# Cross-entropy over 256 x 32000 logits: another order of the row groups and other sizes of the first loads

## The chip, the cores and the metric

The kernel runs on one core of one Trainium2 chip. The metric is the device time of one execution in microseconds (us). Three executions of the kernel before took 82.39, 82.45 and 82.46 us, median 82.45 us.

## The reference

```python
def setup_inputs():
    batch, num_classes = 256, 32000
    return {
        "logits": np.random.randn(batch, num_classes).astype(np.float32),
        "labels": np.random.randint(0, num_classes, size=batch).astype(np.int32),
    }

def reference(logits, labels):
    log_probs = logits - np.max(logits, axis=-1, keepdims=True)
    log_probs = log_probs - np.log(np.sum(np.exp(log_probs), axis=-1, keepdims=True))
    return np.array([-log_probs[i, labels[i]] for i in range(batch)]).astype(np.float32)
```

For each of the 256 rows the result is log(sum of exp(row)) minus the logit at the row's label. The logits are 32.77 MB of float32, and each of them is read once.

## The kernel before

**Groups and loads.** The 256 rows are cut into four consecutive groups (`GROUPS`, L18). A group of k rows is spread over all 128 partitions: each row is cut into q = 128/k equal pieces, and each piece takes one partition, so that a group of 128 rows has 32000 columns per partition, one of 64 rows has 16000 and one of 32 rows has 8000. All groups together have 64000 columns per partition, and one such column over 128 partitions is 512 bytes. Each group is loaded in a few pieces of consecutive columns (`LOADS`, L20). The loads are numbered through all groups, x0 to x13; x8 to x13 lie side by side in one tile, `x_tail`.

**Buffers.** x0 to x5 each have a buffer of their own (`SLOTS`, L30), and their loads are issued at the start, one after the other, on SP's queue (`load`, L204 to L206). x0's load is moved ahead of the barrier at the program's start. x6 and x7 use the buffers of two earlier loads again, and `x_tail` (`TAIL_SLOT`, L32) that of a third one. Their loads are issued on the same queue, each once the work on the buffer's former contents is over. The order is written out by hand: the loop at L307 to L312 places each later load behind the steps that free its buffer.

**Steps.** For each load, `step` (L270) runs `exps` (L215) on ACT: an exponential in place over the whole load, 128 partitions x its columns. What sums its result differs:

- For the loads of the first group, ACT sums along the row itself, into one column of `parts`. After the group's last load, DVE adds these columns (L284), and a matmul with the group's columns of `weights` brings the 128 partition sums to one sum per row (L285).
- For the loads in `HALVED` (L41: x2 to x11), DVE adds the two halves of the result and sums them (L294), and a matmul adds that to the group's sums (L300).
- For the last two, x12 and x13, ACT sums itself again, and the matmul at L300 follows directly.

**Weights.** `weights` says which partitions belong to which row, each entry times exp(-logit at the label). The logits at the labels are gathered by indirect DMAs near the start (L250); the exponential of them (L274) is placed on ACT behind the exponential of load number `GATHERED` (L39), and L276 to L282 make the weights from it. The logarithm of weights times sums is then the result itself.

**End.** The logarithms (`logs`, L222) run on ACT: that of the first group behind the second group's first exponential, those of the middle groups and of the last group at the end, from two banks of PSUM. Then SP stores the 256 results (L318). 16 matmuls whose result is not used (L291, `WARM`) are placed behind the exponential of x7.

Of the kernel before, what the change touches and what calls it, by code (L numbers as in the profile page):

```python
# [14 lines left out]

GROUPS = [64, 128, 32, 32]  # L18

LOADS = [  # L20
    [2048, 13952],
    [8896, 8192, 8320, 6592],
    [4736, 3264],
    [2496, 1824, 1344, 992, 736, 608],
]
CHUNKS = [n for ns in LOADS for n in ns]
GROUP_OF = [g for g, ns in enumerate(LOADS) for _ in ns]


SLOTS = [0, 1, 2, 3, 4, 5, 2, 3]  # L30
TAIL = len(SLOTS)
TAIL_SLOT = 1  # L32
SKIP = 32


WARM_FROM = 7
WARM = 16

GATHERED = 1  # L39

HALVED = range(2, 12)  # L41


def begin_first_load_before_barrier(nc):
# [72 lines left out]
def kernel(  # L117
# [9 lines left out]
    B, C = logits.shape  # L127
    assert B == P * ROWS == sum(GROUPS)
    row_at = [sum(GROUPS[:g]) for g in range(len(GROUPS) + 1)]
    for k, ns in zip(GROUPS, LOADS):  # L130
        assert P % k == 0 and sum(ns) * P == k * C
    assert C % (P // min(GROUPS)) == 0


    flat = [
        logits[row_at[g]:row_at[g + 1], :].rearrange("k (q c) -> (k q) c", q=P // k)
        for g, k in enumerate(GROUPS)
    ]
    starts = [sum(ns[:j]) for ns in LOADS for j in range(len(ns))]
    first_of = [GROUP_OF.index(g) for g in range(len(GROUPS))]  # L140
    last_of = [first_of[g] + len(ns) - 1 for g, ns in enumerate(LOADS)]
# [6 lines left out]
    width = {}  # L148
    for i, s in enumerate(SLOTS):
        width[s] = max(width.get(s, 0), CHUNKS[i])  # L150
    width[TAIL_SLOT] = max(width[TAIL_SLOT], sum(CHUNKS[TAIL:]))


    place = []
    for i, s in enumerate(SLOTS):
        skip = SKIP if s == 0 else 0
        t = big.tile([P, skip + width[s]], F32, name=f"x{i}", tag=f"slot{s}")
        place.append(t[:, skip:skip + CHUNKS[i]])
    assert all(width[s] % 64 == 0 for s in width)
    tail = big.tile([P, width[TAIL_SLOT]], F32, name="x_tail", tag=f"slot{TAIL_SLOT}")  # L160
    for i in range(TAIL, last + 1):
# [3 lines left out]

    assert HALVED[0] == last_of[0] + 1 and HALVED[-1] == last - 2
    assert all(CHUNKS[i] % 2 == 0 for i in HALVED)
    parts = small.tile([P, len(LOADS[0])], F32, name="parts")
    row_0 = small.tile([P, 1], F32, name="row_0")
    near = {i: small.tile([P, 1], F32, name=f"near{i}") for i in range(HALVED[0], last + 1)}  # L170
    res = small.tile([1, B], F32, name="res")
# [36 lines left out]
    def exps(i):  # L208
        if i in HALVED:
            acc = None  # L210
        elif i > last_of[0]:
            acc = near[i][:, :]
        else:
            acc = parts[:, i:i + 1]
        nc.scalar.activation(out=place[i], in_=place[i], func=AF.Exp, accum_out=acc)  # L215
# [8 lines left out]
    with tc.manual_schedule():  # L224
        first = len(set(SLOTS))
        for i in range(first):
# [43 lines left out]
        def step(i):  # L270
            exps(i)
            g = GROUP_OF[i]
            if i == GATHERED:
                nc.scalar.activation(out=eg[:, :], in_=g_at[:, :], func=AF.Exp, scale=-1.0)  # L274
                for r in range(ROWS):
                    nc.vector.tensor_scalar_mul(diag[r][:, :], ident[:, :], eg[:, r:r + 1])  # L276

                for r in range(ROWS):
                    nc.tensor.matmul(  # L279
                        spread[:, r * P:(r + 1) * P], ones[:, :], diag[r][:, :], start=True, stop=True  # L280
                    )
                nc.vector.tensor_mul(out=weights[:, :], in0=holds[:, :], in1=spread)  # L282
            if i == last_of[0]:
                nc.vector.reduce_sum(out=row_0[:, :], in_=parts[:, :], axis=mybir.AxisListType.X)  # L284
                nc.tensor.matmul(lane[0], row_0[:, :], weigh(0), start=True, stop=True)  # L285
            if i == last_of[0] + 1:
                logs(slice(0, row_at[1]), lane[0])
            if i == WARM_FROM:
                col = place[i][:, CHUNKS[i] - 1:CHUNKS[i]]
                for _ in range(WARM):  # L290
                    nc.tensor.matmul(warm, col, diag[0][:, :], start=True, stop=True)  # L291
            if i in HALVED:
                half = CHUNKS[i] // 2
                nc.vector.scalar_tensor_tensor(  # L294
                    out=place[i][:, 0:half], in0=place[i][:, 0:half], scalar=1.0,
                    in1=place[i][:, half:CHUNKS[i]],
                    op0=mybir.AluOpType.mult, op1=mybir.AluOpType.add, accum_out=near[i][:, :],
                )
            if g:
                nc.tensor.matmul(  # L300
                    lane[g], near[i][:, :], weigh(g), start=i == first_of[g], stop=i == last_of[g]
                )


        assert GATHERED <= last_of[0]
        done = 0
        for i in range(first, last + 1):  # L307
            slot = SLOTS[i] if i < TAIL else TAIL_SLOT
            while done <= SLOTS[:first].index(slot):
                step(done)  # L310
# [40 lines left out]
```

## Time and profile before

| what | value |
|---|---|
| median of the three executions | 82.45 us |
| profiled execution, its own time | 82.39 us |
| its span, first to last instruction | 80.8 us |
| busy: ACT, DVE, PE | 57.5, 27.6, 11.6 us |
| the 32.77 MB of the logits' queue, as a share of 16 DMA engines' span | 95.1% |
| exponential of 128x13952, 128x8896, 128x608 | 11829, 7601, 693 ns |
| starts of the exponentials of x1, x3, x4, x5 | 21.27, 41.42, 51.23, 59.02 us |
| DVE's half additions at L294, all ten | 25.9 us |

Times within a profile count from the start of its span. The time of the profiled execution is 1.6 us above its span, for what lies around the instructions. In a group's line, after the name of the operation and its shapes, stand the number of its instructions, then their busy time and the mean duration of one, and then the idle time of the engine just ahead of them with the work that ended it. In the chain of work that ended last, each piece is released by the one before it.

### The profile page before, as it was taken

The numbers are of one execution on the slowest core, as the hardware profiler recorded it, in microseconds if no ns is written. First come the engines' busy times: TensorE is split into PE (matmuls) and PEld (weight loads), VectorE is DVE, ScalarE is ACT, GpSimd is POOL, SyncE is SP. The second block draws the span as 40 slices with busy tenths as digits, with TensorE's granted clock in tenths as the row PEclk, the third lists the DMA queues.
The fourth block names the chain that finished last, engine by engine and source line by source line (L and its number), as shares of the span: only waits on it lengthen the run. The fifth ranks groups of instructions, "written<-read, shape, count | busy, mean of one in ns | idle before, by whom it ended". The sixth has DMA issues, their size and how long they took to land.

```text
span 80.8 us, 261 instructions
## 1 busy us (share of the span) xinstructions
PE 11.6 (14%) x66; PEld 6.3 (8%) x66; DVE 27.6 (34%) x28; ACT 57.5 (71%) x23; POOL 5.2 (6%) x20
## 2 busy tenths in 40 slices
PE   0040000000000000240000200020000201159961
PEld 0040000000000000220000000000000000036630
DVE  1020000000000000220079509920099198898870
ACT  6063000000499999999979990699979999999993
POOL 4006950000000000000000000000000000000000
PEclk9999999999999999999999999999999999999999
DMA  5988989999969798998998996999999999999940
GB/s 134 580 387 359 442 387 442 442 442 442 564 282 564 317 529 373 406 519 373 406 527 346 445 527 290 444 457 444 413 413 422 421 427 421 420 415 420 407 179 1
DMA packets 2084, 32.77 MB, mean 406 GB/s; under 512 B 290, under 2 KB 291, under 8 KB 932
## 3 DMA queue, kind: packets, MB, share of 16 engines
q1 hardware_dynamic: 2018, 32.77, 95.1%
q0 software_dynamic: 64, 0.00, 0.1%
q10 hardware_dynamic: 2, 0.00, 0.0%
HBM read 32.77 MB, written 0.00 MB: 406 GB/s over the span
## 4 chain that ended last, share of the span: by engine, by line
DMA 61%; ACT 34%; SPq 2%; another core or an unknown queue 1%; issue 1%; PE 0%
DMA x<-in_logits_dram 61%; ACT x L215 24%; ACT x_tail L215 9%; SPq L206 2%; PE bank L300 0%; ACT res L222 0%
## 5 line engine op out<-in xcount | busy, mean ns | idle before, releaser
L215 ACT ACTIVATE x<-x 128x2048 f32<-128x2048 f32 (+7 forms) x8 | 48.1, 6032 | 21.1 <-DMA x<-in_logits_dram 21.1
L294 DVE SCALAR_TENSOR_TENSOR x<-x 128x4448 f32<-128x4448 f32 (+5 forms) x6 | 21.8, 3631 | 16.1 <-ACT x L215 16.1
L276 DVE TENSOR_SCALAR diag<-ident,eg 128x128 f32<-128x128 f32 x2 | 0.5, 286 | 27.4 <-ACT eg L274 27.4
L300 PE MATMUL bank<-weights,near 128*1 128x32 f32 (+1 forms) x24 | 3.7, 262 | 34.4 <-DVE x L294 33.2
L215 ACT ACTIVATE x_tail<-x_tail 128x2496 f32<-128x2496 f32 (+5 forms) x6 | 7.5, 1304 | 0.0
L291 PE MATMUL bank<-diag,x 128*1 128x128 f32 x32 | 5.6, 355 | 0.0
L279 PE MATMUL bank<-diag,ones 128*128 128x128 f32 x4 | 1.2, 461 | 27.9 <-DVE diag L276 27.9
L294 DVE SCALAR_TENSOR_TENSOR x_tail<-x_tail 128x1248 f32<-128x1248 f32 (+3 forms) x4 | 4.1, 1025 | 0.6 <-ACT x_tail L215 0.3
L300 PEld LDWEIGHTS bank<-weights,near 128*1 128x1 f32 x24 | 1.0, 82 | 37.2 <-DVE x L294 35.5
L291 PEld LDWEIGHTS bank<-diag,x 128*1 128x1 f32 x32 | 3.4, 107 | 2.0
L279 PEld LDWEIGHTS bank<-diag,ones 128*128 128x128 f32 x4 | 0.9, 324 | 28.0 <-DVE diag L276 28.0
L250 POOL DMA_INDIRECT g_at<-in_logits_dram,idx x2 | 2.1, 1030 | 0.6 <-issue 0.3
L198 ACT ACT_TABLE_LOAD x1 | 1.3, 1283 | 0.8 <-PEq L335 0.8
L239 PE MATMUL bank<-one,lbl_row 1*128 1x1 f32 x4 | 1.0, 352 | 4.8 <-DVE lbl_row L237 4.8
L237 DVE CAST lbl_row<-words 1x256 f32<-1x256 int32 x1 | 0.3, 281 | 3.4 <-DMA words<-in_labels_dram 3.4
L239 PEld LDWEIGHTS bank<-one,lbl_row 1*128 1x128 f32 x4 | 0.9, 316 | 4.8 <-DVE lbl_row L237 4.8
L265 POOL TENSOR_SCALAR_AFFINE_SELECT holds<-holds 128x32 f32<-128x32 f32 (+2 forms) x4 | 1.0, 238 | 0.3
L261 POOL TENSOR_SCALAR_AFFINE_SELECT holds<-holds 128x32 f32<-128x32 f32 (+2 forms) x4 | 1.0, 238 | 0.1
L282 DVE TENSOR_TENSOR weights<-holds,bank 128x256 f32<-128x256 f32 x1 | 0.4, 420 | 1.2 <-PE bank L279 1.2
L222 ACT ACTIVATE res<-bank 1x64 f32<-1x64 f32 (+2 forms) x3 | 0.7, 219 | 0.1
L242 DVE CAST lbl<-bank 128x2 int32<-128x2 f32 x1 | 0.2, 159 | 1.1 <-PE bank L239 1.1
L294 DVE DVE_READ_ACCUMULATOR x<-x 128x1 f32 x6 | 0.5, 83 | 0.0
(18 smaller groups left out, 3.7 us busy)
## 6 DMA issues: line engine op xcount, KB each, us to landing
x<-in_logits_dram SPq DMA_DIRECT2D x1, 6976.0 KB, 20.4
x<-in_logits_dram SPq DMA_DIRECT2D x1, 4448.0 KB, 30.6
x<-in_logits_dram SPq DMA_DIRECT2D x1, 4160.0 KB, 48.9
x<-in_logits_dram SPq DMA_DIRECT2D x1, 4096.0 KB, 39.7
x<-in_logits_dram SPq DMA_DIRECT2D x1, 3296.0 KB, 56.2
x<-in_logits_dram SPq DMA_DIRECT2D x1, 2368.0 KB
x<-in_logits_dram SPq DMA_DIRECT2D x1, 1632.0 KB, 15.6
x_tail<-in_logits_dram SPq DMA_DIRECT2D x1, 1248.0 KB
```

The lines of the kernel that those rows point to most:

```text
L198: nc.scalar.preload_act_table_set("natural_log_exp_and_others")
L206: nc.sync.dma_start(out=place[i], in_=flat[GROUP_OF[i]][:, a:a + CHUNKS[i]])
L215: nc.scalar.activation(out=place[i], in_=place[i], func=AF.Exp, accum_out=acc)
L222: nc.scalar.activation(out=res[0:1, rows], in_=sums, func=AF.Ln)
L239: nc.tensor.matmul(lbl_up[:, r:r + 1], lbl_row[:, r * P:(r + 1) * P], one[:, :], start=True, stop=True)
L250: nc.gpsimd.indirect_dma_start(out=g_at[:, r:r + 1], out_offset=None, in_=logits[:, :], in_offset=bass.IndirectOffsetOnAxis(ap=idx[:, r:r ...
L261: nc.gpsimd.affine_select(out=h, in_=h, pattern=[[-q, k]], base=0, channel_multiplier=1, compare_op=mybir.AluOpType.is_ge, fill=0.0,)
L265: nc.gpsimd.affine_select(out=h, in_=h, pattern=[[q, k]], base=q - 1, channel_multiplier=-1, compare_op=mybir.AluOpType.is_ge, fill=0.0,)
L279: nc.tensor.matmul(spread[:, r * P:(r + 1) * P], ones[:, :], diag[r][:, :], start=True, stop=True)
L291: nc.tensor.matmul(warm, col, diag[0][:, :], start=True, stop=True)
L294: nc.vector.scalar_tensor_tensor(out=place[i][:, 0:half], in0=place[i][:, 0:half], scalar=1.0, in1=place[i][:, half:CHUNKS[i]], op0=mybir. ...
L300: nc.tensor.matmul(lane[g], near[i][:, :], weigh(g), start=i == first_of[g], stop=i == last_of[g])
```

## The change

The group of 128 rows comes first, ahead of the one of 64. The first group thus has four loads instead of two, 1024, 5120, 12992 and 12864 columns, and the second group two instead of four. There are 14 loads as before. The first six have 48000 columns together in both kernels. `HALVED` begins at x4 instead of x2: ACT sums for x0 to x3, and DVE has eight halves to add instead of ten. x6 takes the buffer of x1, x7 that of x3 as before, and `x_tail` that of x2. The logits at the labels are taken in behind x2's exponential. The sizes of the loads of the later groups change by little. Of the functions nothing changes.

```diff
-GROUPS = [64, 128, 32, 32]
+GROUPS = [128, 64, 32, 32]

 LOADS = [
-    [2048, 13952],
-    [8896, 8192, 8320, 6592],
-    [4736, 3264],
-    [2496, 1824, 1344, 992, 736, 608],
+    [1024, 5120, 12992, 12864],
+    [9216, 6784],
+    [4608, 3392],
+    [2560, 1824, 1312, 960, 736, 608],
 ]
...
-SLOTS = [0, 1, 2, 3, 4, 5, 2, 3]
+SLOTS = [0, 1, 2, 3, 4, 5, 1, 3]
 TAIL = len(SLOTS)
-TAIL_SLOT = 1
+TAIL_SLOT = 2
...
-GATHERED = 1
-
-HALVED = range(2, 12)
+GATHERED = 2
+
+HALVED = range(4, 12)
```

## The prediction

> **What bounds the kernel now.** I began with the page's slices and its chain of waits.
>
> ```profile
> ACT  6063000000499999999979990699979999999993
> DMA  5988989999969798998998996999999999999940
> DMA x<-in_logits_dram 61%; ACT x L215 24%; ACT x_tail L215 9%; SPq L206 2%; PE bank L300 0%; ACT res L222 0%
> ```
>
> The last line says whose work the chain consists of: loads, then ACT. The DMA row is full almost from end to end; ACT's is full only from the 11th slice on, with one hole. The chain in order of time shows where the one hands over to the other.
>
> ```profile
> 51.23 7.14 ACT x L215
> 58.37 0.62 another core or an unknown queue
> 59.02 5.62 ACT x L215
> 64.68 3.88 ACT x L215
> 68.74 2.91 ACT x L215
> 71.64 7.46 ACT x_tail L215 x8
> 79.15 0.23 PE bank L300 x2
> 79.41 0.19 ACT res L222
> ```
>
> From 59.02, the start of x5's exponential, ACT runs without a pause to the end; ahead of it ACT waited 0.62 us for x5's load. So the end is x5's landing plus what ACT has left. Two stretches of the windows view confirm that both are full at once there.
>
> ```profile
> 1.00:77.90 76.90, 11.05 (x60) 6.09 (x60) 27.05 (x26) 55.76 (x18) 4.87 (x16) 1.00 1.00 426
> 59.02:77.90 18.88, 7.27 (x46) 3.99 (x46) 15.69 (x15) 18.88 (x8) 0.00 (x0) 1.00 0.99 416
> ```
>
> The columns are stretch, length, busy time of PE, its weight load, DVE, ACT and POOL, clock, share of the DMA engines, GB/s. The DMA engines are busy from 1.00 to 77.90 (share 1.00), and ACT is busy for all 18.88 us of the second stretch. The groups by shape give durations and releasers.
>
> ```profile
> L215 ACT ACTIVATE x<-x 128x13952 f32<-128x13952 f32 x1 | 11.8, 11829 | 14.6 <-DMA x<-in_logits_dram 14.6
> L215 ACT ACTIVATE x<-x 128x8896 f32<-128x8896 f32 x1 | 7.6, 7601 | 0.0
> L215 ACT ACTIVATE x<-x 128x8320 f32<-128x8320 f32 x1 | 7.1, 7137 | 2.8 <-DMA x<-in_logits_dram 2.8
> L294 DVE SCALAR_TENSOR_TENSOR x<-x 128x4448 f32<-128x4448 f32 x1 | 4.8, 4793 | 5.3 <-ACT x L215 5.3
> L215 ACT ACTIVATE x_tail<-x_tail 128x608 f32<-128x608 f32 x1 | 0.7, 693 | 0.0
> ```
>
> ACT's pauses are ended by loads, never by DVE; DVE waits for ACT.
>
> **Two rates.** The exponentials that a load released start at 21.27 (16000 columns loaded by then), 41.42 (33088), 51.23 (41408) and 59.02 (48000). That is 1.179, 1.179 and 1.182 ns per column: the stream takes 1.18 ns. ACT takes (7601 - 693)/(8896 - 608) = 0.8335 ns per column. From the start of 8896 (33.19 in the timeline) to the next instruction (40.70) is 7.51 us, 0.10 above 8896 columns. An accumulator read adds 0.09 (33.01 to 33.10).
>
> **What costs nothing.** DVE loses the halves of x2 and x3, 4.8 and 4.4 us, and PE their two matmuls; ACT's work never waits for them, so this is worth 0. x6 no longer waits on SP for DVE at 45.66 but for x1's exponential, at about 14; behind it on SP's queue x7 waits for x3's exponential, at about 51, not for DVE until 52.95; the tail's loads stand behind that. The stream reaches x7 only after 52608 columns, at about 64.5, so 13 us cover both; with that cover gone each us late would be a us at the end. x2 lands at about 24.97 and takes 11.03 with its read, plus 0.09 for L274: ACT is free at 36.1, 4 us ahead of x3. The weights and the first group's matmul move to 51.1 to 52; the logarithm that needs them comes at 58.8. DVE adds x4's halves (4608 columns, about 5 us) while x5's exponential takes 5.8, and stays within ACT's pace from there; its last half ends about 0.8 us ahead of ACT's last sum. The middle logarithm has 96 columns instead of 160. By the rows of 64 and 160 (196 and 276 ns) that is 0.05 less, but it ended at 79.28 and the last logarithm had to wait for PE until 79.38: saved 0.
>
> **ACT from x3 on.** x3 comes with 32000 columns: 41.42 - 1088 x 1.18 ns = 40.14. Its 12864 columns and read take 11.83 (21.27 to 33.10, for 13952) less 0.91 = 10.92, to 51.06. x4 (41216 columns) lands at 51.00, so a pause of 2.78 us is used up and ACT is 0.06 behind. x4 takes 7.51 + 320 x 0.8335 ns = 7.78, to 58.84. The first group's logarithm, now 128 columns and placed here, takes 0.25 by the rows above, less the 0.09 by which ACT's instructions overlap: 59.00. x5 lands at 59.02 as before (48000 columns). Three pauses of before (2.78, 0.65 and 0.53) are down to 0.02.
>
> **ACT from x5 on.** 22784 columns instead of 22592: 192 x 0.8335 ns = +0.16. One thing goes: from x5's start to x6's was 5.66, which is 0.17 above its columns, where the next two have 0.11 and 0.09. The chain shows why: x6's load (52736 columns, about 64.6) came as ACT became free. Now x6 has 52608 columns and lands 0.15 earlier while ACT comes 0.1 later: -0.06. The sum is +0.10.
>
> **Two terms that can only add.** First, the chain x3, x4, logarithm, x5 has no room left: any landing of x3 a little late against x5's, or a dearer logarithm, is at once at the end. Bounds: 0, and 0.2 (the 0.09 overlap not had and the 0.1 by which a rate of 1.182 in place of 1.179 shifts 32000 columns). I take 0.05, near the lower end, since the three rates agree that well. Second, the start: the first load carries 1024 columns, 1.21 us of stream, instead of 2.42. It is issued at 0.00, the next at 0.80, behind the barrier. If the second's data follow its issue as fast as the first's (1.00 us; the windows view shows no byte before), there is no gap, with 0.4 us to spare; where it is slower by more, all of the stream and so the end is late. The trace never shows this delay without a backlog. Bounds: 0, and 1.2 if all of the cover is lost. The nearest row is the first load's own start, so I take 0.04.
>
> The Trainium skill (DMA: Bandwidth & Descriptors, Bandwidth) asks for 1 MiB or more per DMA to reach 75% of the peak, measured there for loads issued from GpSimd, which speaks against a first load of 0.5 MiB. By its fixed 2.0 us for a DMA (Anatomy of one DMA), of which the first load's transfer would cover 1.2, an estimate from it would be 0.8 more, 83.4. In this trace the tail's loads of 368 to 912 KB, queued back to back, ran at 420 and 407 GB/s (the slices from 72.7 to 76.8 us), so I count no such loss.
>
> **Sum.** 0.10 + 0.05 + 0.04 = +0.19. The profiled execution's 82.39 (80.8 of span and 1.6 around it) becomes 82.58; the median is 0.06 above it, so 82.64, or 0.23% more. About 0.2% (0.16 us) is what a measurement can tell from no change.
>
> **Rivals.**
> - *A gap in the stream at the start.* The second load's data come more than 0.4 us later after its issue than the first's did. For it: SP's issues take 0.33, 0.42 and 0.62 us one after the other, so the queue is slower under load. Against it: the shares at 2.0 to 3.0 us are 0.94 and 0.98 right after a start. It gives 82.8 to 83.7, most likely below 83.
> - *The stream runs ahead: not slower.* Between the first landing (4.68) and x1's (21.27) it took 1.189 ns per column; at 1.179 those 13952 columns would take 0.14 less. The place is the stream up to x3, and it decides from 0.03 us on: with x3's exponential starting ahead of 40.11 and x5's ahead of 59.0, the whole chain to the end moves with it. It gives 82.50, in its far part (0.4 us of stream gained) 82.25. For it: only that one stretch; against it: the stretch holds the start itself, and the later rates are the same for pieces of 128-row and 64-row groups.
> - *The bare sum.* Both adding terms are nil, and the end moves by the 0.10 alone: 82.55, within 0.2%. For it: each link closes by the rows above, if only just.
>
> **How the numbers follow.** Forecast (a sum of +0.17 to +0.3): 0.40. Gap: 0.15. Stream ahead: 0.25, of which 0.17 within 0.2% and 0.08 beyond. Bare sum: 0.20, of which 0.15 within and 0.05 faster, should the tail also hide the 192 columns and more. Slower 0.40 + 0.15 = 0.55, same 0.17 + 0.15 = 0.32, faster 0.08 + 0.05 = 0.13. The range takes the near part of the gap and the near part of the stream's gain: 82.38 to 82.98. The forecast's own is 82.62 to 82.75.
>
> **What would show it.** Right: x3 starts near 40.14; x4, the logarithm and x5 follow with pauses of under 0.1; x5 starts at 59.02 to 59.1; the last exponential starts at 78.4 to 78.55 instead of 78.31; the DMA share is near 1.00 from 1.0 to 77.9. A gap: slices with little DMA between 2 and 4 us and all starts late by the same amount. Stream ahead: x3 and x5 both early. Wrong altogether: a pause of ACT after x5, ended by a load or by DVE.

## The result, and the profile after

The changed kernel takes 82.94 us (median of four executions, 82.78 to 83.08), the kernel before beside it 82.43 us (82.39 to 82.46). The ratio is 1.0062, with a 95% interval of 1.0039 to 1.0085: slower by 0.51 us. The forecast was 82.64 in a range of 82.38 to 82.98. The profiled execution took 83.05 us (span 81.4), so it lies 0.11 above the median, in the upper half of a scatter of 0.3 us. Before, the scatter was 0.07 us.

The slices of the page:

```profile
ACT  6320299000004999990099999999999999999993
...
DMA  4999999999999999999797979999999999999910
```

From its first long exponential on, ACT has one pause, 3.99 us ahead of x3; before it had three there (0.53, 2.78 and 0.65 us). No slice of the DMA row stands out at the start: the queue has no gap there. The chain in order of time (start, length, what):

```profile
1.66 39.09 DMA x<-in_logits_dram
...
40.76 18.79 ACT x L215 x3
59.55 0.15 ACT res L222
59.71 5.40 ACT x L215
...
72.34 7.42 ACT x_tail L215 x8
...
79.81 0.23 PE bank L300 x2
...
80.06 0.19 ACT res L222
```

The hand-over from loads to ACT has moved from x5 to x3. From x3's exponential (40.76) ACT runs to the end without a pause, as the forecast had it. What it did not have is that start: 40.14 was worked out, so x3 landed 0.62 us late. The groups by shape show no idle time ahead of x4's exponential and of the logarithm. By the timeline it is 10.93 us from the start of x3's exponential to that of x4's, and 7.77 from there to the logarithm, as worked out (10.92 and 7.78):

```profile
L215 ACT ACTIVATE x<-x 128x12864 f32<-128x12864 f32 x1 | 10.9, 10922 | 4.0 <-DMA x<-in_logits_dram 4.0
L215 ACT ACTIVATE x<-x 128x9216 f32<-128x9216 f32 x1 | 7.9, 7867 | 0.0
...
L222 ACT ACTIVATE res<-bank 1x128 f32<-1x128 f32 x1 | 0.2, 249 | 0.0
```

Where the 0.62 us comes from shows in the last microsecond before the last bytes arrive. The windows view of the kernel before, then of the changed one; the last but one number is the share of time that the 16 DMA engines are busy:

```profile
76.85:77.85 1.00, 0.81 (x12) 0.46 (x10) 0.93 (x3) 1.00 (x2) 0.00 (x0) 1.00 0.81 315
```

```profile
77.47:78.47 1.00, 0.39 (x9) 0.17 (x6) 0.96 (x3) 1.00 (x2) 0.00 (x0) 1.00 0.20 76
```

Before, the engines end nearly together (0.81). In the changed kernel few of them still work in the last microsecond (0.20), while the others have run out of work. The trace's records of single DMA packets say more. For each load they hold 128 packets, one per partition, and 16 of four bytes. They do not name the engine, but they fall into 16 runs, each of eight packets close behind one another and one of four bytes as a completion; I take each run for one engine. x3's exponential starts 0.38 us behind the last of the 16 completions (before, at this position, 0.37), so a load has landed with the last one. Of x3's load (32000 columns), the median engine completes at 39.49 us in the changed kernel. Before, this worked out at 39.54 (40.82 for 33088 columns, less 1088 at 1.18 ns). So the stream as a whole is on time. But the last engine completes at 40.38, 0.89 us behind the median one; before it was 0.22 for the same position. The last engine was 0.30 behind at the end of the first load, 0.38 at x1's end (9.32), and it lost the other 0.51 early in x2: a pause of 0.28 from 11.24 to 11.52, with a gathered row at its end, and a packet that then took 2.15 us instead of 1.92. As it has the same bytes to move as the others, it did not catch up: it is still 0.82 behind at the last load.

One caution on the comparisons that follow: they leave out executions over 1.5% above a kernel's fastest, and of kernels with first loads of 512 or 1024 columns such executions are part of what is studied; the medians count them.

### The profile page after: what moved, and what is told of

It is laid out like the page before. It is cut to its first block, busy times and chain, and to the rows that moved or that the text cites. A ratio compares the mean times of both kernels' runs of the same rounds, so it can differ in the third digit from the quotient of the medians.

```text
span 81.4 us, 251 instructions
## 1 busy us (share of the span) xinstructions
PE 9.9 (12%) x62; PEld 6.0 (7%) x62; DVE 19.0 (23%) x24; ACT 57.5 (71%) x25; POOL 5.2 (6%) x20
## 4 chain that ended last, share of the span: by engine, by line
DMA 48%; ACT 48%; SPq 1%; issue 1%; PE 0%
DMA x<-in_logits_dram 48%; ACT x L215 38%; ACT x_tail L215 9%; SPq L206 1%; ACT res L222 0%; PE bank L300 0%
## 5 line engine op out<-in xcount | busy, mean ns | idle before, releaser
L215 ACT ACTIVATE x<-x 128x1024 f32<-128x1024 f32 (+7 forms) x8 | 48.1, 6030 | 21.8 <-DMA x<-in_logits_dram 21.8
L294 DVE SCALAR_TENSOR_TENSOR x<-x 128x4608 f32<-128x4608 f32 (+3 forms) x4 | 13.1, 3284 | 9.2 <-ACT x L215 9.2
L215 ACT ACTIVATE x_tail<-x_tail 128x2560 f32<-128x2560 f32 (+5 forms) x6 | 7.4, 1299 | 0.0
L291 PE MATMUL bank<-diag,x 128*1 128x128 f32 x32 | 5.1, 338 | 0.1
L300 PE MATMUL bank<-weights,near 128*1 128x32 f32 (+1 forms) x20 | 2.1, 214 | 20.3 <-DVE x L294 18.7
L294 DVE SCALAR_TENSOR_TENSOR x_tail<-x_tail 128x1280 f32<-128x1280 f32 (+3 forms) x4 | 4.1, 1026 | 0.5 <-ACT x_tail L215 0.3
L285 PE MATMUL bank<-weights,row 128*1 128x128 f32 x2 | 0.6, 397 | 13.6 <-DVE row L284 13.6
L222 ACT ACTIVATE res<-bank 1x128 f32<-1x128 f32 (+2 forms) x3 | 0.7, 219 | 0.2 <-PE bank L300 0.2
```

The costliest lines, as they stand in the source:

```text
L222: nc.scalar.activation(out=res[0:1, rows], in_=sums, func=AF.Ln)
L294: nc.vector.scalar_tensor_tensor(out=place[i][:, 0:half], in0=place[i][:, 0:half], scalar=1.0, in1=place[i][:, half:CHUNKS[i]], op0=mybir. ...
L300: nc.tensor.matmul(lane[g], near[i][:, :], weigh(g), start=i == first_of[g], stop=i == last_of[g])
```

## Experiments

Three theories for the late engine were tested: the gathered rows (their small packets stand beside the late engine's longest delay), the order of the groups (rows 128000 bytes apart from the first load on), and the small first load. The twelve kernels ran in three batches of four, each batch on another chip, with its own runs of the kernel before: 82.46, 82.61 and 82.47 us. The expected times count from about 82.46, so those of the second batch are 0.15 too low. Across batches only the ratios can be compared, and what a chip adds to them is not known.

**a_nogather.** The changed kernel without the gather (`g_at` is set to zero, so the logit at the label is left out).

```diff
-        for r in range(ROWS):
-            nc.gpsimd.indirect_dma_start(
...
+        nc.gpsimd.memset(g_at[:, :], 0.0)
```

> The changed kernel without the two indirect DMAs that gather the logits at the labels; zeros stand in their place, so the result lacks that logit. In the trace of the changed kernel the DMA engine that is last to finish each load is 0.38 us behind the median one at x1's end (9.3 us) and 0.89 us behind at x2's end (25.2 us), and stays so; on it, a gathered packet at 11.5 us stands in a pause of 0.28 us, and the next packet took 2.15 us instead of 1.92. Theory 'gather': without it the last engine stays within 0.4 us of the median, x3's exponential starts at 40.2 to 40.35 instead of 40.76, and the time is 82.4 to 82.65. Theory 'small first loads' and theory 'order of the groups': nothing changes, x3 near 40.7, time 82.8 to 83.1.

Measured: 82.85 us (82.34 to 84.86) beside 82.46 of before; ratio 1.0035, 1.0012 to 1.0058. In its profiled execution (83.23) x3's exponential starts at 41.00, and the last engine is already 1.17 us behind the median at x1's end. The late landing of x1 shows in the start of its exponential, here first in the changed kernel, then in a_nogather:

```profile
9.65 4.47 ACT L215 ACTIVATE x<-x 128x5120 f32<-128x5120 f32 x1 [5.07 <-DMA x<-in_logits_dram]
```

```profile
10.44 4.47 ACT L215 ACTIVATE x<-x 128x5120 f32<-128x5120 f32 x1 [5.84 <-DMA x<-in_logits_dram]
```

So the loss needs no gather. Whether the gather adds to it is open: the interval overlaps that of the changed kernel, in whose profile the larger part of the delay stands beside a gathered row.

**a_first2048.** The changed kernel with the first load of before.

```diff
-    [1024, 5120, 12992, 12864],
+    [2048, 4096, 12992, 12864],
```

> The changed kernel with the first load of before: 2048 and 4096 columns in place of 1024 and 5120, all else as changed. The gather then runs about 1.3 us later, as before. Theory 'small first loads': the spread of the engines goes back to that of before, x3's exponential starts at 40.15 to 40.3, and the time is 82.5 to 82.65. Theory 'order of the groups': x3 stays near 40.7 and the time at 82.8 to 83.1. Theory 'gather': in between or unchanged, since the gathered packets still come in x2, 82.6 to 83.1.

Measured: 82.54 us (82.41 to 82.64); ratio 1.0007, 0.9998 to 1.0017. The chain:

```profile
1.65 38.64 DMA x<-in_logits_dram
...
40.32 18.79 ACT x L215 x3
59.11 0.16 ACT res L222
59.27 5.43 ACT x L215
```

x3's exponential starts at 40.32, a little above the expected 40.15 to 40.3, and the time is as the theory of the small first load had it. All but 0.08 us of the 0.51 goes with the first load's size (the interval does not meet the changed kernel's, 1.0039 to 1.0085), and the scatter goes too.

**order_only.** The order of the groups alone, with large first loads.

```diff
-    [1024, 5120, 12992, 12864],
+    [2048, 13952, 8896, 7104],
...
-SLOTS = [0, 1, 2, 3, 4, 5, 1, 3]
+SLOTS = [0, 1, 2, 3, 4, 5, 2, 3]
-TAIL_SLOT = 2
+TAIL_SLOT = 1
```

> The order 128, 64, 32, 32 alone: the first group's loads are 2048, 13952, 8896 and 7104 columns, the first three sizes being those of before; buffers are reused as before (x6 in x2's, x7 in x3's, the tail in x1's). ACT has 4 us of room ahead of x4 here, so that only landings and the 192 columns from x5 on can move the end. Theory 'order of the groups' (rows 128000 bytes apart from the start spread the engines): x5's exponential starts 0.4 us or more later than 59.02, time 82.8 or more. Theories 'small first loads' and 'gather' (gathered packets of 2 us neighbours in x1, as before): x5 at 58.95 to 59.1, time 82.45 to 82.6.

Measured: 82.47 us (82.36 to 82.92); ratio 1.0005, 0.9991 to 1.0019. The chain:

```profile
50.99 7.88 ACT x L215
58.87 0.16 ACT res L222
59.03 5.41 ACT x L215
```

The order is worth nothing that could be measured, either way.

**b_first1024.** The kernel before with a small first load.

```diff
-    [2048, 13952],
+    [1024, 14976],
```

> The kernel before with first loads of 1024 and 14976 columns instead of 2048 and 13952. Theory 'small first loads': the engines spread as in the changed kernel, x5's exponential starts 0.3 us or more later than 59.02, time 82.7 or more. Theory 'order of the groups': as before, 82.4 to 82.5. Theory 'gather': the gathered packets come 1.3 us earlier, into the first or second packets of 2.2 us; 82.4 to 83.0 by chance of which engine is hit. A gap at the start (the rival of the forecast) would also show here, as x1 landing later than 21.3.

Measured: 83.14 us (82.88 to 84.93); ratio 1.0113, 1.0069 to 1.0156. In this batch the first load alone makes the old order slower by more than the whole change did. x5's exponential starts at 59.65 instead of 59.02:

```profile
59.65 12.64 ACT L215 ACTIVATE x<-x 128x6592 f32<-128x6592 f32 x3 [0.64 <-DMA x<-in_logits_dram]
```

Two engines are late. By the packet records their first packet of x1 took 3.07 and 3.02 us, where the usual one takes 2.21. One of the six initial issues on SP's queue is long too (operation, number, shortest, median and longest duration in ns):

```profile
L206 SPq DMA_DIRECT2D x<-in_logits_dram x8: 328/411/978, 0.0 to 53.8; - x8
```

The longest issue, x5's, took 978 ns instead of 448 for x5's before (616 was the longest there). It ran from 2.62 to 3.60, while the two long packets did; that it waited for their engines is not shown.

So the first load's size is the cause, and what it costs is time of single engines: over x1's packets in the profiles of a_nogather and b_first1024, but only 0.08 of 0.89 us there in that of the changed kernel. The next eight kernels asked why, and from which size on. Two theories stood against each other. 'Short lead': x1's data come too soon behind x1's own issue. 'Later issues': the queue is given x2 to x5 while x1's data already run.

**a_first512.** Still less in the first load.

```diff
-    [1024, 5120, 12992, 12864],
+    [512, 5632, 12992, 12864],
```

> The changed kernel with first loads of 512 and 5632 columns. x0's data end at about 2.0 us. Theory 'short lead': worse than 1024, 83.1 to 83.8, with x1's packets slow from its start or even a pause of the whole queue ahead of them. Theory 'later issues': about as with 1024 or worse, 82.9 to 83.4. If the loss does not depend on the first load's size, 82.5 to 82.7.

Measured: 83.02 us (82.62 to 85.08) beside 82.61 of before, 0.5% more by the medians; ratio 1.0032, 1.0012 to 1.0053. The profiled execution is one of the longest (85.07, where eight of the eleven took 82.62 to 83.28). ACT's timeline and the last microsecond of its loads:

```profile
2.76 0.63 ACT L215 ACTIVATE x<-x 128x512 f32<-128x512 f32 x1 [0.68 <-DMA x<-in_logits_dram]
...
12.27 4.90 ACT L215 ACTIVATE x<-x 128x5632 f32<-128x5632 f32 x1 [8.79 <-DMA x<-in_logits_dram]
```

```profile
79.46:80.46 1.00, 0.37 (x9) 0.16 (x5) 0.96 (x3) 1.00 (x2) 0.00 (x0) 1.00 0.06 25
```

x1's exponential starts at 12.27 instead of 9.65, and at the end one engine of 16 works alone (share 0.06). Its first packet of x1 came at 3.94 and took 2.03 us instead of 0.84. Here the first packets of x1 on the other engines are long too, mostly 0.9 to 1.5 us: they start at 2.0 to 2.7 us and get through at 3.2 to 3.7. The packets fit 'short lead' best: an engine that comes to x1's packets early has to wait for something. The time does not decide: less the 0.15 of this batch the median is 82.87, just below the ranges of both.

**a_first1536.** Half way.

```diff
-    [1024, 5120, 12992, 12864],
+    [1536, 4608, 12992, 12864],
```

> The changed kernel with first loads of 1536 and 4608 columns (1024 and 5120, 2048 and 4096 are measured: 82.94 and 82.54). x1's data start at about 3.3 us, behind x0. Both theories 'later issues' (the last issue ends at 3.1 to 3.3) and 'short lead' expect most of the loss gone: 82.5 to 82.7. If what counts is only that the first load be large, half of it: 82.7 to 82.8.

Measured: 82.86 us (82.76 to 82.94) beside 82.61; ratio 1.0028, 1.0019 to 1.0038. That is 0.25 us. Less the 0.15 of this batch the time is 82.71, on the border of the two ranges (82.5 to 82.7, and 82.7 to 82.8 for 'only that the first load be large'), so it does not decide. Its profiled execution shows no long packets of x1 at all; its engines are spread by 0.56 us from the end of the first load on. This run I can't explain by waits within x1.

**a_hold.** The loads of x3 to x5 issued behind x0's exponential.

```diff
-SLOTS = [0, 1, 2, 3, 4, 5, 1, 3]
+SLOTS = [0, 1, 2, 0, 4, 5, 1, 0]
...
-        first = len(set(SLOTS))
+        first = 3
...
-            while done <= SLOTS[:first].index(slot):
+            held = [j for j in range(min(i, TAIL)) if SLOTS[j] == slot]
+            while held and done <= held[-1]:
```

> The changed kernel, with the loads of x3, x4 and x5 issued only behind x0's exponential (about 4.6 us) instead of at 1.66 to 3.1 us; for that x3 takes x0's buffer. x1 and x2 are issued as before and feed the queue until 25 us. So far the first load's 1024 columns are what costs: on one to three of the 16 DMA engines the packets of x1 take up to 1 us longer, and every later landing waits for these engines. Theory 'later issues' (the queue is being given x2 to x5 while x1's data already run, 2.6 us on, which with 2048 columns happens before x1 starts): the loss goes or moves, x5's exponential starts at 59.0 to 59.2, time 82.45 to 82.7. Theory 'short lead' (x1 itself starts too soon behind its own issue at 0.80): no change, 82.8 to 83.1.

Measured: 82.70 us (82.57 to 82.94) beside 82.61; ratio 1.0012, 1.0000 to 1.0024. Taken alone this speaks for 'later issues'. But the changed kernel did not run in this batch, so what it loses on this chip is not known.

**a_two_early.** x1's issue, too, ahead of the barrier.

```diff
-    first = next(i for i in rest if i.engine == mybir.EngineType.SP and i.opcode == "DMACopy")
-    rest.remove(first)
+    first = [i for i in rest if i.engine == mybir.EngineType.SP and i.opcode == "DMACopy"][:2]
+    rest = [i for i in rest if i not in first]
...
-    head.insert(at, first)
+    head[at:at] = first
```

> The changed kernel with x1's load, too, issued ahead of the barrier, right behind x0's (about 0.45 us instead of 0.80); the other four initial loads move up by 0.35 us with it. Theory 'short lead': x1 has as much more time, the engines stay within 0.4 us of each other, time 82.45 to 82.65. Theory 'later issues': their last one ends at 2.7 instead of 3.1 us, still behind x1's start at 2.6; half of the loss is left, 82.6 to 82.9.

Measured: 82.78 us (82.60 to 82.92) beside 82.61; ratio 1.0015, 1.0002 to 1.0028. The two comparisons' intervals overlap with each other and with that of a_first2048. My working of the issues was wrong in one thing: behind two issues ahead of the barrier, the next comes at 1.27, not earlier, and the last of the six ends at 3.26. So x1's lead grew by 0.35 us while the later issues moved further into x1's time, and the loss was still small. By this argument the run speaks for 'short lead' and against 'later issues'. Its time alone does not: less the 0.15 it is 82.63, in the ranges of both.

To decide between them, and because the scatter is large, the last batch ran the same two edits on the old order with a small first load, beside that kernel and the changed one.

**after_again** is the changed kernel.

> The changed kernel itself, beside the three kernels that follow, since the earlier comparisons ran on two chips. Expected 82.8 to 83.0 where the kernel before takes 82.43 (0.4 to 0.7% more); less only if the loss of the first load differs from chip to chip.

Measured: 82.81 us (82.56 to 83.74) beside 82.47; ratio 1.0046, 1.0019 to 1.0074. Its profiled execution (82.66) is one of the quick ones, with the last engine 0.28 us behind the median at x3's end: the same kernel has it 0.89 behind in one execution and hardly at all in another.

**b1024_again** is b_first1024.

> The kernel before with first loads of 1024 and 14976 columns, once more, as the reference for the next two: it took 1.1% more than before (82.88 to 84.93). Expected 0.5 to 1.5% more again.

Measured: 82.70 us (82.50 to 83.94); ratio 1.0031, 1.0015 to 1.0046. Slower again, but by less than in the first batch (1.0113); the intervals do not meet, so the loss differs from batch to batch, and each batch had another chip.

**b1024_hold**: the edits of a_hold, with `SLOTS = [0, 1, 2, 0, 4, 5, 2, 0]`.

> The kernel before with first loads of 1024 and 14976, and the loads of x3, x4 and x5 issued only behind x0's exponential (x3 takes x0's buffer). Theory 'first load's size alone': the loss stays, 0.5 to 1.5%. Theory 'later issues' and theory 'both together' (x1's data start within 2 us of its issue, and the queue is being given more loads then): the loss is gone, within 0.2% of before, no engine more than 0.5 us behind the median.

Measured: 83.37 us (four executions, 82.88 to 83.89); ratio 1.0130, 1.0070 to 1.0190. The loss stays, so it does not need the issues of x3 to x5 at the start of x1's data. One engine's first packet of x1 took 2.81 us instead of 2.21. It ran from 2.99 to 5.80, and the held issues came at 4.66, 5.03 and 5.53, still in x1's time: the edit moves them and does not take them out. Why a_hold, with the same edit, lost only 0.12% stays open.

**b1024_two_early**: the edit of a_two_early.

> The kernel before with first loads of 1024 and 14976, both issued ahead of the barrier. The later issues then end at 3.26 us, still behind x1's start at about 2.7. Theory 'later issues' alone: the loss stays. Theory 'short lead' and theory 'both together': the loss is gone or under 0.25%. Theory 'first load's size alone': it stays, 0.5 to 1.5%.

Measured: 82.57 us (82.42 to 82.82); ratio 1.0010, 1.0000 to 1.0021. By the medians the earlier issue of x1 takes the loss from 0.23 to 0.10 us. The two intervals overlap a little (1.0015 to 1.0021), so this is likely and not shown. In its profile (82.82) the last engine is 0.58 behind at x1's end, but 0.62 at the end of x0 already: x1 added nothing.

| kernel | first load | x1 issued at | time against before | x1's packets above the usual duration, sum over the engines, profiled execution | last engine behind the median at the end of x0, of x1 |
|---|---|---|---|---|---|
| before | 2048 | 0.80 | 1 | 0.59 us | 0.28, 0.25 us |
| order_only | 2048 | 0.80 | 1.0005 | 0.55 us | 0.18, 0.15 us |
| a_first2048 | 2048 | 0.80 | 1.0007 | 0.10 us | 0.48, 0.45 us |
| a_first1536 | 1536 | 0.80 | 1.0028 | 0.01 us | 0.37, 0.37 us |
| changed kernel | 1024 | 0.80 | 1.0062 | 1.39 us | 0.30, 0.38 us |
| after_again (changed kernel) | 1024 | 0.80 | 1.0046 | 0.35 us | 0.33, 0.31 us |
| a_nogather | 1024 | 0.80 | 1.0035 | 2.92 us | 0.29, 1.17 us |
| b_first1024 | 1024 | 0.80 | 1.0113 | 4.11 us | 0.22, 0.74 us |
| b1024_again (b_first1024) | 1024 | 0.80 | 1.0031 | 2.95 us | 0.15, 0.78 us |
| a_hold | 1024 | 0.80 | 1.0012 | 0.13 us | 0.32, 0.30 us |
| b1024_hold | 1024 | 0.80 | 1.0130 | 3.21 us | 0.23, 0.48 us |
| a_two_early | 1024 | 0.45 | 1.0015 | 0.06 us | 0.37, 0.37 us |
| b1024_two_early | 1024 | 0.45 | 1.0010 | 1.51 us | 0.62, 0.58 us |
| a_first512 | 512 | 0.80 | 1.0032 (median 1.005) | 6.88 us | 0.24, 2.49 us |

The last column tells the kernels apart better than the sum, which is 0.59 before without any loss. With 1536 or 2048 columns, or with x1 issued at 0.45, the last engine falls back no further over x1. With 1024 or 512 columns and x1 issued at 0.80 it falls back by 0.25 to 2.2 us in five of eight profiles, by 0.08 in the changed kernel's and not at all in two.

Shown: with a first load of 1024 columns or fewer whose second load is issued at 0.80, the time is 0.3 to 1.3% longer in every kernel but a_hold (0.12%); with 2048 columns all but 0.1% of it goes; in the profiles the loss sits in single DMA engines. Likely, but not shown: that an issue of the second load at 0.45 takes it away as well (0.10 and 0.15% are left). Open: what such an engine waits for, why it strikes one execution and not the next, why a_hold escapes it, and the 0.25 us of 1536 columns. No kernel here beats the kernel before. Both loads issued early together with a first load of 2048 was not tried; order_only, where the engines are close together already, leaves it little to gain.

## Why the prediction was right or wrong

**Direction and range: right; the forecast's size: too small.** 0.51 us came instead of 0.19. The failing step is the second of the "two terms that can only add", the start, for which I took 0.04 from bounds of 0 and 1.2. Undoing the first load's size alone takes the excess from 0.51 to 0.08 us, so that term is 0.43 by this comparison of two batches. On the old order a first load of 1024 cost 0.26 and 0.93 us (b1024_again and b_first1024). Nor was 1.2 its upper bound: three of the nine executions of b_first1024 took 83.95 to 84.05, about 1.5 us above before.

**Why the term was mis-sized.** I asked whether the queue as a whole would run dry, and the answer to that was right: it does not, and the median engine is on time to 0.05 us. But a load lands with its last engine, and I had not asked for each engine. That 1.21 us of stream covers 0.80 of issue on average and not on each of 16 engines is my reading; the runs make it likely and do not show it. The first load's own packets held the hint: its first packets took 0.36 to 0.86 us in the trace of before, where later ones took 0.31. The windows view showed that as shares of 0.78 between 1.5 and 2.0 us, and I read it as a matter of the start alone. The nearest row for a second load close behind its issue was the first load itself, with this tail, and not its earliest byte at 1.00.

**The gap rival** had the right place and direction (82.8 to 83.7), and its price held. Its mechanism, a pause of all of the stream with slices of little DMA between 2 and 4 us, did not come; it took the form of a few late engines. So that the median lies in the range is partly luck: the range reached up to 82.98 only for this rival, and two of the four executions (83.05 and 83.08) lie above it.

**The links x3, x4, logarithm, x5** held to 0.02 us. x3's exponential and read took 10.93 (worked out 10.92), and x4's exponential with the logarithm 7.94 (51.69 to 59.63, worked out 7.94). x5 landed just as ACT became free. So the 0.05 taken there was not needed: the chain passed x3's delay on and added nothing of its own.

**From x5 on**, the forecast was +0.10. From x5's start to the last exponential's it is 19.34 us (59.63 to 78.97) against 19.30 (59.02 to 78.31), +0.04. The 192 columns and the pause ahead of x6 are there as worked out. The rest is small change: before, the exponential of x6 and three of the tail stood some 0.015 us longer each, for their columns, than they do now, and I read that as their loads coming just as ACT became free, which I did not test.

**The bare sum** was the case closest to the change without its first load: a_first2048 has +0.08 us, with an interval of -0.02 to 0.14, where that rival had 0.10.

**The stream runs ahead**: no run had it. x3 never started ahead of 40.11 in any profile that has x3 at 32000 columns and ACT free for it.

**What was costed at nothing** cost nothing: x6 issued at 14.2 and x7 at 51.8 in the trace after, no idle time of ACT ended by DVE, and the last logarithm waited for PE (80.04) with the shorter middle one done by then (79.88).

**The skill's rules.** The Trainium skill (DMA: Bandwidth & Descriptors, Bandwidth) asks for 1 MiB per DMA. The first load of 0.5 MiB did cost, though not as a fixed time that is laid open: the estimate from that page, 83.4, was too high for the median, and b_first1024 passed it in single executions. The same page's section on latency (Latency and other measured facts) gives about 0.6 us to the first byte of a DMA issued from SP. It does not say from where it counts: here the first packet starts at 1.02 us, that is 1.02 behind the start of the first issue and 0.62 behind its end. An estimate by that figure has x1's data free to flow from 1.4 us on, or from 1.7 if it counts from the end of the issue, and no engine would have to wait for it. The runs show no such fixed time: with 512 columns first, x1's first packets start at 2.0 to 2.7 us and mostly need 0.9 to 1.5 us instead of 0.84. The measurement decides.

## What to carry to other kernels

A load lands with the slowest of the DMA engines that share it, and where each engine has a fixed share of every load (here eight of 128 packets) and the queue never runs dry, an engine that loses time once stays late to the end (0.89 us behind at 25 us, 0.82 at the last load). So a mean share near 1.00 does not say that landings are on time: compare the share in the last microsecond ahead of the last landing. Size the first load so that each engine's part of it outlasts the second load's issue by a good margin (here 2048 columns, 2.4 us, against an issue at 0.80), or try an earlier issue of the second load, and measure such a start over many executions, since one can show nothing (82.56) and the next 1 us more (83.74).

## What the runs showed of the hardware that was not expected

- With the first load at 512 columns, one engine of 16 had its first packet of the second load finished at 5.97 us, where the others had theirs at 3.2 to 3.7, and it kept those 2.3 us to the end of the kernel: the last bytes came at 80.46 while the other engines were done at about 78.4.
- In some executions with a late engine the last of the six initial issues was long: 1585 ns with 512 columns, and 978, 1043 and 701 ns in the profiled executions of b_first1024, a_nogather and b1024_again, against 448 before. It is no sure sign: in the changed kernel, with its late engine, it took 459, and in after_again, without one, the fifth issue took 650.
- Long packets are not only the first ones of the second load: in the changed kernel an engine's packet at 11.52 us took 2.15 us instead of 1.92, behind a pause of 0.28 with a gathered row in it. Without the gather (a_nogather) the time was 0.35% longer than before all the same.
